# A hybrid decoder layer on one core: late visits of staged pieces in pairs, two more staging buffers, a shorter Newton step, and a residual added by a matrix product

## The chip, the core and the metric

The kernel runs on one core of a Trainium2 chip. A core has TensorE (PE in the profile, with its weight loads as PEld), VectorE (DVE), ScalarE (ACT), GpSimd (POOL) and SyncE (SP); the last three also issue DMAs. The metric is the device time of one execution in microseconds (us); lower is better.

## What is computed

One inference step of a decoder layer, in fp32, for 256 prompt tokens and for 8 sequences with 4 new tokens each (32 decode rows), so 288 tokens in all:

```
h = rms_norm(x, g)                        # 288 x 2048
z = h @ w_in                              # columns of three head groups and their gates
y_conv = silu(c_g) * short_conv(...)      # 512 wide
o_cmp, o_sel, o_win = sparse attention    # 8 heads, 2 kv groups; compressed, selected, window
y_nsa = silu(n_g) * (g0*o_cmp + g1*o_sel + g2*o_win)
y_mem = silu(m_g) * attend(m_q, memory)   # 4 heads, 256 memory tokens
x = x + concat(y_conv, y_nsa, y_mem) @ w_out
y = rms_norm(x, final_g)
```

The 8 decode sequences have 2048 past tokens each in a paged cache, 512 window rows and 256 memory tokens. These are read from HBM once: keys for compression, selected keys and values, window keys and values, memory keys and values. New key and value rows, the updated window and the convolution state are outputs as well.

## The kernel before, in words

**The main stream.** TensorE works through one long list of products of a 1024-column half of a weight tile with the activations (tiles `z`). Each fp32 operand is split into a high part and a rest (`wh` and `wl` for weights), and three of the four partial products are formed, so that one half costs 24 matmuls of 128x128 by 288 columns (`product_half`). A weight half is loaded by GpSimd's DMA queue (`w_load`, L225) into one of five buffers, ScalarE makes `wh` of it and VectorE `wl`. The halves come in the order of `wsrc`: memory projection, input projection, output projection.

**Work between the products.** Every 12 matmuls the program calls `chunk()`, which lets a set of generators each issue a little: softmaxes, transposes, gates, and the visits of staged pieces. The order on every engine is therefore fixed when the program is built. A generator goes on when a small clock `at` says so, which is advanced by estimated costs (`Timed`, `matmul`, `loading`).

**Staged pieces.** The caches of the decode rows come in pieces of 128x1024 (512 KB). `stages` lists them by due time, `load_next` issues a load whenever a buffer is free, and `stage_stream` visits a stage when all four of its pieces are there by the estimate: it runs 16 small matmuls (output 32 rows by 256 columns) and returns the four buffers with `used_up`, which issues the next loads. There are six buffers `st` and, once the prompt's memory attention is over, a seventh in the tile `qk1`. Visits of the second half of the sequences late in the kernel are: selected keys 7 (`selk_use`, tile `sk`), window keys (`wink_use`, `sk` and `sn`), memory values 0 and 1 (`memv_use`, tile `omd`), window values (`winv_use`, tile `od`), selected values 4 to 7 (`selv_use`, `od`). A value visit first transposes the next part of the softmax weights on TensorE (`weights`, tile `pv`) and then multiplies with the part made a visit earlier. The selected values are gathered by GpSimd with an indirect DMA (L584), on the same queue as the weights.

**Order around these visits.** When both halves are through, `dec_out` writes the decode rows of `mixed`, and `split_decode` prepares them. After twelve first passes of the output projection, four weight halves are multiplied the other way round (`first_rows`, tiles `zr`), then the second passes follow.

**The tail.** The last 512 output columns are held by rows: two groups of 128 prompt tokens (`part[0]`, `part[1]`) and the decode rows, folded as 128x128 (`part[2]`, product tile `zd`). For each group the squares are summed, `factors` computes 1/sqrt with ScalarE's Sqrt, VectorE's reciprocal and one Newton step (`rsqrt` with `rest`), ScalarE scales the rows, TensorE spreads the factors over the partitions (`rb`), and VectorE scales the twelve column tiles (`scale_tiles`).

## Time and profile before

| what | value |
|---|---|
| time, median of 3 runs | 613.99 us (611.5 to 619.14) |
| profiled execution, its own time | 616.16 us |
| its span, first to last instruction | 614.4 us |
| granted TensorE clock, mean | 0.996 |
| PE busy | 603.0 us (98%) |
| DVE busy | 461.0 us (75%) |
| ACT busy | 285.3 us (46%) |
| POOL busy | 200.5 us (33%) |
| HBM traffic over the span | 323 GB/s |

Times in the rows are microseconds from the start of the span. A row of the timeline has start, length, engine, line, operation, output<-inputs, shapes, the number of records, and in brackets the engine's idle time ahead of it with what ended it. One fp32 matmul leaves two records, a product matmul of the main stream one. Matmuls are pipelined: the length of a row is longer than its share of the engine, so shares are read from one start to the next. Lines such as L120 or L137 are the helpers that issue a matmul or an operation of VectorE or ScalarE, so that the tile names tell more.

### The profile page before, as it was taken

The page shows a single profiled execution, that of the slowest core. Times are in us where ns is not written, and L with a number is a line of the kernel's source. Part 1 is how long each engine was busy: PE and PEld are TensorE (multiplying, and loading weights), DVE is VectorE, ACT ScalarE, POOL GpSimd, SP SyncE. Part 2 cuts the span into 40 slices and gives each one's busy share as a digit, 9 for nine tenths or more (in the row PEclk, how much of TensorE's full clock was granted, in tenths as well). Part 3 has the DMA queues.
Part 4 walks back from the last instruction along what each step waited for, and adds up shares of the span by engine and source line. Part 5 has one row for each costly group of instructions (what it writes and reads, how often), then busy time and mean ns, then how long its engine had stood idle before and what let it go on. Part 6 is the DMA issues. An engine that isn't in the chain of part 4 may idle for free.

```text
span 614.4 us, 13419 instructions
## 1 busy us (share of the span) xinstructions
PE 603.0 (98%) x4919; PEld 554.0 (90%) x4919; DVE 461.0 (75%) x749; ACT 285.3 (46%) x499; POOL 200.5 (33%) x282
## 2 busy tenths in 40 slices
PE   8999999999999999999999999999999999999997
PEld 5999999989799999989889889899889989889995
DVE  4879899988485779989789888897668733357666
ACT  4755445543355444435334434543543544335552
POOL 2012544533124442433453552323111336222200
PEclk8999999999999999999999999999999999999999
DMA  8999798999968999798878898999899998859834
GB/s 285 394 403 404 258 320 300 345 310 337 365 203 280 370 407 375 250 387 298 310 232 313 284 386 273 309 318 311 289 334 332 336 353 291 288 195 411 281 130 155
DMA packets 76226, 190.85 MB, mean 311 GB/s; under 512 B 8896, under 2 KB 26464, under 8 KB 75904
## 3 DMA queue, kind: packets, MB, share of 16 engines
q0 software_dynamic: 26048, 100.48, 46.0%
q1 hardware_dynamic: 49104, 88.25, 40.4%
q10 hardware_dynamic: 1008, 1.25, 0.6%
q8 instruction: 39, 0.64, 0.4%
q14 instruction: 27, 0.22, 0.1%
HBM read 184.74 MB, written 13.60 MB: 323 GB/s over the span
## 4 chain that ended last, share of the span: by engine, by line
PE 78%; DMA 11%; DVE 8%; issue 2%; SPq 1%; ACT 0%; ACTq 0%; DVEq 0%
PE z L120 56%; DMA st<-ckc 5%; PE zr L120 4%; PE od L120 3%; DMA st<-ckk 3%; PE sk L120 3%; PE zf L120 2%; DVE wl L137 2%; DVE pooled L137 2%; PE acc L120 2%; PE s L120 2%; DMA rx<-xT 1%; DVE st L137 1%; PE pt L125 1%; DMA mraw<-memT 1%
## 5 line engine op out<-in xcount | busy, mean ns | idle before, releaser
L120 PE MATMUL z<-x,wh 128*128 128x288 f32 x1664 | 254.4, 302 | 0.0
L137 DVE TENSOR_TENSOR wl<-w,wh 128x1024 fp32r<-128x1024 f32 x147 | 185.7, 1265 | 84.6 <-PE z L120 34.9
L120 PEld LDWEIGHTS z<-x,wh 128*128 128x128 f32 x1664 | 229.7, 188 | 7.8 <-issue 6.1
L137 ACT ACTIVATE wh<-w 128x1024 fp32r<-128x1024 f32 x148 | 154.3, 1052 | 25.1 <-PE z L120 15.4
L120 PE MATMUL z<-x,wl 128*128 128x288 f32 x832 | 127.2, 295 | 0.3 <-DVE wl L137 0.3
L120 PEld LDWEIGHTS z<-x,wl 128*128 128x128 f32 x832 | 115.7, 188 | 0.8 <-DVE wl L137 0.7
L356 POOL TENSOR_TENSOR st<-st,cst 128x512 f32<-128x512 f32 x63 | 69.3, 1102 | 133.8 <-DVE st L137 49.3
L225 POOL DMA_DIRECT2D w<-w_in x104 | 58.2, 560 | 109.1 <-DVE wl L137 82.4
L137 DVE TENSOR_REDUCE pooled<-st 128x16 f32<-128x1024 f32 x63 | 76.2, 1210 | 5.8 <-POOL st L356 5.8
L137 DVE TENSOR_TENSOR st<-st,cst 128x512 f32<-128x512 f32 x63 | 43.3, 688 | 10.9 <-DMA st<-ckc 10.8
L225 POOL DMA_DIRECT2D w<-w_out x32 | 17.5, 550 | 63.0 <-DVE wl L137 43.1
L584 POOL DMA_INDIRECT st<-ckv,rows_v x26 | 27.1, 1042 | 31.9 <-PE od L120 17.4
L137 ACT ACTIVATE P<-P,nm 128x128 f32<-128x128 f32 (+1 forms) x32 | 14.2, 445 | 29.3 <-DVE nm L137 29.3
L120 PE MATMUL z<-m,wh 128*128 128x256 f32 x192 | 27.3, 287 | 0.5 <-DVE mvt L137 0.5
L120 PE MATMUL z<-y,wh 128*128 128x288 f32 x192 | 27.6, 297 | 0.0
L120 PE MATMUL z<-y1a,wh 128*128 128x288 f32 x168 | 26.7, 299 | 0.0
L120 PEld LDWEIGHTS z<-y,wh 128*128 128x128 f32 x192 | 26.3, 188 | 0.1
L120 PEld LDWEIGHTS z<-y1a,wh 128*128 128x128 f32 x168 | 23.6, 188 | 2.1 <-issue 1.2
L120 PEld LDWEIGHTS z<-m,wh 128*128 128x128 f32 x192 | 24.7, 191 | 0.8 <-issue 0.7
L120 PE MATMUL sk<-st,qz 128*32 128x256 f32 x272 | 20.4, 383 | 1.4 <-DMA st<-ckk 1.2
L120 PE MATMUL od<-st,S 128*32 128x256 f32 x256 | 18.7, 382 | 0.0
L120 PE MATMUL zf<-mixed,w 128*128 128x256 f32 x64 | 16.6, 421 | 1.9 <-DVE mixed L137 1.7
(318 smaller groups left out, 716.2 us busy)
## 6 DMA issues: line engine op xcount, KB each, us to landing
w<-w_in POOLq DMA_DIRECT2D x104, 512.0 KB
st<-ckc SPq DMA_DIRECT2D x126, 256.0 KB, 5.8
w<-w_out POOLq DMA_DIRECT2D x32, 512.0 KB
st<-ckk SPq DMA_DIRECT2D x112, 128.0 KB, 5.1
w<-w_mem SPq DMA_DIRECT2D x12, 512.0 KB, 7.1
o_wk<-wk POOLq DMA_DIRECT2D x8, 512.0 KB
o_wv<-wv POOLq DMA_DIRECT2D x8, 512.0 KB
st<-mv SPq DMA_DIRECT2D x7, 512.0 KB, 7.9
```

The costliest lines, as they stand in the source:

```text
L120: nc.tensor.matmul(out, a, b, **kw)
L125: nc.tensor.transpose(out, a, b)
L137: return getattr(self.engine, name)(*args, **kw)
L225: (nc.gpsimd if s >= ON_SYNC else nc.sync).dma_start(raws[s], wsrc[s])
L356: done.append(eng.tensor_tensor(tm[:, :, kv], tm[:, :, kv], acmp[:, kv].unsqueeze(1).unsqueeze(1).to_broadcast([128, 2, 4, 64]), op=ALU.mu ...
L584: nc.gpsimd.indirect_dma_start(t, None, ckv, bass.IndirectOffsetOnAxis(ap=rows_v[:, j * 4 + b:j * 4 + b + 1], axis=0))
```

## The change

**Pairs.** `HELD` names four stages of the second half. When `stage_stream` reaches one of them it keeps it back and visits it together with the next stage: selected keys 7 with the window keys, memory values 0 with 1, selected values 4 with 5, and 6 with 7. Before a pair of value visits both parts of the softmax weights that it still needs are transposed. The buffers of both stages come free together.

**Two more buffers.** When the prompt's attention is over and the first half of the sequences is decoded, the new keys that are still needed are copied out of `kk` (a VectorE copy of 128x128 into columns 3712 to 3840 of `qk1`), and columns 0 to 1024 and 2176 to 3200 of `qk1` are given to the staging as buffers eight and nine.

**Newton step.** In the tail, the step multiplies r*r by v in one operation of VectorE, where two stood, with the factor -0.5 taken into a second set of constants (`rest` has six columns, written by one more small operation).

**Residual of the decode rows.** The residual `part[2]` is no longer added by VectorE: a matmul with the identity puts it into `zd` ahead of the decode products, and the squares and the gains read `zd` directly.

```diff
--- before.py
+++ after.py
@@ -199,11 +199,15 @@
     def rsqrt(r, ssq, rest=None):
 
         v, t = small(3, "yv", 1)[:, :r.shape[1]], small(3, "yt", 1)[:, :r.shape[1]]
-        act.activation(r, ssq, AF.Sqrt, scale=1.0 / D, bias=C("eps") if rest is None else rest)
-        if rest is None:
-            vec.tensor_scalar(v, ssq, 1.0 / D, EPS, op0=ALU.mult, op1=ALU.add)
-        else:
-            vec.scalar_tensor_tensor(v, ssq, 1.0 / D, rest, op0=ALU.mult, op1=ALU.add)
+        if rest is not None:
+            act.activation(r, ssq, AF.Sqrt, scale=1.0 / D, bias=rest[0])
+            vec.scalar_tensor_tensor(v, ssq, -0.5 / D, rest[1], op0=ALU.mult, op1=ALU.add)
+            vec.reciprocal(r, r)
+            vec.scalar_tensor_tensor(t, r, r, v, op0=ALU.mult, op1=ALU.mult)
+            vec.scalar_tensor_tensor(r, t, 1.5, r, op0=ALU.add, op1=ALU.mult)
+            return
+        act.activation(r, ssq, AF.Sqrt, scale=1.0 / D, bias=C("eps"))
+        vec.tensor_scalar(v, ssq, 1.0 / D, EPS, op0=ALU.mult, op1=ALU.add)
         vec.reciprocal(r, r)
         vec.tensor_tensor(t, r, r, op=ALU.mult)
         vec.scalar_tensor_tensor(t, t, -0.5, v, op0=ALU.mult, op1=ALU.mult)
@@ -481,7 +485,7 @@
             for g in range(2):
                 for b in range(4):
                     matmul(s[32 * b:32 * b + 32, 32 * j:32 + 32 * j], qcols(0, 4 * hf + b, g),
-                                     kk[:, 2 * j + g, 256:288], start=(g == 0), stop=(g == 1), skip_group_check=True)
+                                     kn[hf][:, 2 * j + g], start=(g == 0), stop=(g == 1), skip_group_check=True)
         nmask = C("newmask")[:, hf * 32:(hf + 1) * 32]
         vec.tensor_tensor(S[:, C_NS:C_NS + 32], s[:, 0:32], nmask, op=ALU.add)
         vec.tensor_tensor(S[:, C_NW:C_NW + 32], s[:, 32:64], nmask, op=ALU.add)
@@ -567,7 +571,7 @@
     def values(hf, i, t):
 
         o, PT = env["o"], env["PT", hf, i]
-        if i < 4:
+        if i < 4 and ("PT", hf, i + 1) not in env:
             weights(hf, i + 1)
         t = [x.rearrange("p (n c) -> p n c", n=4) for x in t]
         for n in range(4):
@@ -726,6 +730,7 @@
     tiles_of, ready, place = {}, {}, {}
     buffers = [one.tile([128, 1024], F32, name=f"st{i}") for i in range(NST)]
     free = []
+    HELD = ((selk_use, 7), (memv_use, 0), (selv_use, 4), (selv_use, 6))
     nl = [0]
 
     def load_next():
@@ -747,15 +752,26 @@
 
         last_cmp = 0.0
         needs = {selk_use: "q", memk_use: "mq"}
+        held = []
         for due, f, u, j in stages:
             while (now[0] < due - EARLY or needs.get(u) not in env or len(tiles_of.get((u, j), ())) < pieces(u) or at[0] < ready[u, j]
                    or u is cmp_use and (at[0] < last_cmp + CMP_GAP or at[VEC] > at[0] + BACKLOG)):
                 yield 1
             if u is cmp_use:
                 last_cmp = at[0]
-            yield from u(j, tiles_of.pop((u, j)))
+            if (u, j) in HELD:
+                held.append((u, j))
+                continue
+            if u is selv_use and held:
+                for q in (j % 4 + 1, j % 4 + 2):
+                    if q < 5 and ("PT", j // 4, q) not in env:
+                        weights(j // 4, q)
+            for u, j in (*held, (u, j)) if u is not cmp_use else ((u, j),):
+                yield from u(j, tiles_of.pop((u, j)))
+                if u is not cmp_use:
+                    used_up(u, j)
             if u is not cmp_use:
-                used_up(u, j)
+                held.clear()
 
 
     m_hl = [xhl.tile([128, KT, 256], F32R, name=f"m{n}", tag=f"qk{n}") for n in range(2)]
@@ -1343,6 +1359,12 @@
                 yield from prompt_nsa(g, tt)
                 yield 1
         env["prompt_done"] = True
+        while not env.get(("decoded", 0)):
+            yield 1
+        vec.tensor_copy(kn[1], kk[:, :, 256:NT])
+        for o in (0, 2176):
+            free.append(qk1[:, o:o + 1024])
+            load_next()
 
 
     def then(gen):
@@ -1363,6 +1385,7 @@
     qq = xhl.tile([128, 16, 256], F32, name="qq", tag="qk0")
     qk1 = xhl.tile([128, 4096], F32, name="qk1", tag="qk1")
     kk = qk1[:, 0:4 * NT].rearrange("p (i n) -> p i n", i=4)
+    kn = [kk[:, :, 256:NT], qk1[:, 3712:3840].rearrange("p (i n) -> p i n", i=4)]
     mq = qk1[:, 1152:2176].rearrange("p (h t) -> p h t", h=4)
     vnat = {3: qk1[:, 2176:2688].rearrange("p (s g d) -> p s g d", s=2, g=2),
             5: qk1[:, 2688:3200].rearrange("p (s g d) -> p s g d", s=2, g=2)}
@@ -1528,7 +1551,7 @@
     yo = xhl.tile([128, 4096], F32, name="yo", tag="qk1")
     yod = pbig.tile([128, 1024], F32, name="yod", tag="big")[:, :512]
     out = (yo[:, 0:2048], yo[:, 2048:4096], yod)
-    rest, sums2 = small(3, "yrest", 1), small(3, "ysums", 1)
+    rest, sums2 = small(6, "yrest", 1), small(3, "ysums", 1)
     quarters = small(32, "imp", 1)
     both = zt("A", "both")
     sel, accd = both[:, 0:128], both[:, 128:256]
@@ -1546,18 +1569,21 @@
             for q in range(4):
                 o = (k % 2) * ROWS + 128 * q
                 matmul(zd[32 * q:32 * q + 32, :128], mixed[:, k, 256:NT], wr[k // 2][:, o:o + 128],
-                       start=(k == 0), stop=(k == KT - 1), skip_group_check=True)
-
-    def squares(g, z):
-        vec.tensor_tensor(part[g], z, part[g], op=ALU.add)
-        act.activation(scratch[:, :part[g].shape[1]], part[g], AF.Square, accum_out=sums2[:, g:g + 1])
+                       start=False, stop=(k == KT - 1), skip_group_check=True)
+
+    y_of = [part[0], part[1], zd[:, :128]]
+
+    def squares(g):
+        if g < 2:
+            vec.tensor_tensor(part[g], z[g], part[g], op=ALU.add)
+        act.activation(scratch[:, :part[g].shape[1]], y_of[g], AF.Square, accum_out=sums2[:, g:g + 1])
 
     def gains(g):
-        vec.tensor_tensor(out[g][:, out[g].shape[1] - part[g].shape[1]:], part[g], fgr[g], op=ALU.mult)
+        vec.tensor_tensor(out[g][:, out[g].shape[1] - part[g].shape[1]:], y_of[g], fgr[g], op=ALU.mult)
 
     def factors(g, ssq):
         r = small(1, f"yr{g}", 1)
-        rsqrt(r, ssq, rest[:, g:g + 1])
+        rsqrt(r, ssq, (rest[:, g:g + 1], rest[:, 3 + g:4 + g]))
         return r
 
     def spread_rows(g, r):
@@ -1598,8 +1624,9 @@
     for i, a in enumerate((acc[:, 0:128], acc[:, 128:256], accd)):
         matmul(ssq[:, i:i + 1], a, C("ones"), start=True, stop=True, skip_group_check=True)
     rows(z[0], ws[2], 6, y, 0, False, True)
-    vec.tensor_scalar(rest, ssq[:, 0:3], 1.0 / D, EPS, op0=ALU.mult, op1=ALU.add)
-    squares(0, z[0])
+    vec.tensor_scalar(rest[:, 0:3], ssq[:, 0:3], 1.0 / D, EPS, op0=ALU.mult, op1=ALU.add)
+    vec.tensor_scalar(rest[:, 3:6], ssq[:, 0:3], -0.5 / D, -0.5 * EPS, op0=ALU.mult, op1=ALU.add)
+    squares(0)
     gains(0)
     r0 = factors(0, sums2[:, 0:1])
     scale_rows(0, r0, nc.sync)
@@ -1609,16 +1636,17 @@
     rows(z[1], ws[2], 6, y, 1, False, True)
     scale_tiles(0, 0, 4, nc.sync)
     scale_tiles(0, 4, 8, nc.sync)
-    squares(1, z[1])
+    squares(1)
     scale_tiles(0, 8, 12, nc.sync)
     gains(1)
     r1 = factors(1, sums2[:, 1:2])
     scale_rows(1, r1, nc.scalar)
+    matmul(zd[:, :128], ident, part[2], start=True, stop=False, skip_group_check=True)
     decode_rows(0, SPREAD_AT)
     spread_rows(1, r1)
     decode_rows(SPREAD_AT, KT)
     scale_tiles(1, 0, 4, nc.sync)
-    squares(2, zd[:, :128])
+    squares(2)
     busy(TAIL_BUSY[0])
     matmul(ssq[:, 3:4], sel, sums2[:, 2:3], start=True, stop=True)
     scale_tiles(1, 4, 8, nc.sync)
```

On GpSimd's queue, the weight loads (`w`) and the gathers of selected values (`st` and `qk` from `ckv`) stand as follows before, from the weight loads ahead of the third group of gathers on:

```order
L225 DMA w_6472<-w_out 128x1024
L225 DMA w_6506<-w_out 128x1024
L584 DMA st_105<-ckv,rows_v 128x1024
L584 DMA st_107<-ckv,rows_v 128x1024
L584 DMA st_106<-ckv,rows_v 128x1024
L584 DMA st_109<-ckv,rows_v 128x1024
L225 DMA w_6566<-w_out 128x1024
L225 DMA w_6600<-w_out 128x1024
L584 DMA st_108<-ckv,rows_v 128x1024
L584 DMA st_104<-ckv,rows_v 128x1024
L584 DMA qk_793<-ckv,rows_v 128x1024
L584 DMA st_105<-ckv,rows_v 128x1024
```

With the change, from the fourth weight load after the second group of gathers on:

```order
L229 DMA w_6543<-w_out 128x1024
L229 DMA w_6577<-w_out 128x1024
L588 DMA st_109<-ckv,rows_v 128x1024
L588 DMA st_108<-ckv,rows_v 128x1024
L588 DMA st_104<-ckv,rows_v 128x1024
L588 DMA qk_793<-ckv,rows_v 128x1024
L588 DMA st_105<-ckv,rows_v 128x1024
L588 DMA qk_793<-ckv,rows_v 128x1024 x2
L229 DMA w_6660<-w_out 128x1024
L229 DMA w_6692<-w_out 128x1024
```

Groups of four gathers with two or three weight loads between them have become groups of up to seven, with five weight loads ahead of this one.

On TensorE, the first of the two memory value visits (tile `omd`) stands before between products `z` in this way, and the second follows 60 products later:

```order
L120 MATMUL z_6098<-x_112,wh_6014 128x288
L120 MATMUL z_6098<-x_113,wh_6014 128x288
L120 MATMUL omd<-st_106,qk_793 32x256 x4
L120 MATMUL omd<-st_109,qk_793 32x256 x4
L120 MATMUL omd<-st_108,qk_793 32x256 x4
L120 MATMUL omd<-st_104,qk_793 32x256 x4
L120 MATMUL z_6098<-x_112,wh_6014 128x288
L120 MATMUL z_6098<-x_113,wh_6014 128x288
```

With the change:

```order
L120 MATMUL z_6103<-x_112,wl_6094 128x288 x8
L120 MATMUL omd<-qk_793 32x256 x4
L120 MATMUL omd<-st_107,qk_793 32x256 x4
L120 MATMUL omd<-st_106,qk_793 32x256 x4
L120 MATMUL omd<-st_109,qk_793 32x256 x4
L120 MATMUL omd<-st_108,qk_793 32x256 x4
L120 MATMUL omd<-st_104,qk_793 32x256 x4
L120 MATMUL omd<-qk_793 32x256 x4
L120 MATMUL omd<-st_105,qk_793 32x256 x4
L120 MATMUL z_6219<-x_112,wh_6104 128x288
```

Both visits now stand in one piece, with no product between them, and they come after a full half. The scores against the compressed keys (`sc`, 8 matmuls), which stood right behind the visit of selected keys 7, now stand alone between products, 36 products ahead of the pair of key visits.

At the end of VectorE's list, from the first scaling of the second group's column tiles (`yo` from `ysum` and `rb`) on, there stands before:

```order
L137 TENSOR_TENSOR yo<-ysum,rb 128x512
L137 TENSOR_TENSOR ysum<-zd,ysum 128x128
L137 TENSOR_TENSOR yo<-ysum,rb 128x512
L137 TENSOR_TENSOR yod<-ysum,st_104 128x128
L137 TENSOR_TENSOR yo<-ysum,rb 128x512
L137 SCALAR_TENSOR_TENSOR yv<-ssqy,yrest 128x1
L137 RECIPROCAL yr_7625<-yr_7625 128x1
L137 TENSOR_TENSOR yt<-yr_7625 128x1
L137 SCALAR_TENSOR_TENSOR yt<-yt,yv 128x1
L137 SCALAR_TENSOR_TENSOR yr_7625<-yt,yr_7625 128x1
L137 TENSOR_TENSOR yod<-ysum,rb 128x384
```

With the change:

```order
L137 TENSOR_TENSOR yo<-ysum,rb 128x512 x2
L137 TENSOR_TENSOR yod<-zd,st_104 128x128
L137 TENSOR_TENSOR yo<-ysum,rb 128x512
L137 SCALAR_TENSOR_TENSOR yv<-ssqy,yrest 128x1
L137 RECIPROCAL yr_7625<-yr_7625 128x1
L137 SCALAR_TENSOR_TENSOR yt<-yr_7625,yv 128x1
L137 SCALAR_TENSOR_TENSOR yr_7625<-yt,yr_7625 128x1
L137 TENSOR_TENSOR yod<-ysum,rb 128x384
```

The addition into `ysum` and one operation of the step are gone, and the gain of the decode rows (`yod`) reads `zd`.

## The prediction

> **What bounds the kernel now.** I read the profile's page first, then the busy time by stretches, then the timeline of TensorE where the visits move, then the tail on all engines. The page and the stretches say this:
>
> ```profile
> PE 603.0 (98%) x4919; PEld 554.0 (90%) x4919; DVE 461.0 (75%) x749; ACT 285.3 (46%) x499; POOL 200.5 (33%) x282
> PE z L120 56%; DMA st<-ckc 5%; PE zr L120 4%; PE od L120 3%; DMA st<-ckk 3%; PE sk L120 3%; PE zf L120 2%; DVE wl L137 2%; DVE pooled L137 2%; PE acc L120 2%; PE s L120 2%; DMA rx<-xT 1%; DVE st L137 1%; PE pt L125 1%; DMA mraw<-memT 1%
> 450.00:500.00 50.00, 50.00 (x485) 45.17 (x478) 33.67 (x80) 22.69 (x40) 12.69 (x19) 1.00 0.93 339
> 500.00:550.00 50.00, 50.00 (x419) 44.18 (x418) 20.26 (x21) 21.12 (x33) 18.13 (x25) 1.00 0.75 262
> ```
>
> The reader is to see that TensorE has no idle time from 450 to 550 us (the second and third column: 50.00 of 50.00), where all the moved visits lie, at a granted clock of 1.00, while the DMA engines are busy 93% and 75% of it at 339 and 262 GB/s. There the time is TensorE's list of instructions and what it loses between them. A change of the order can gain only what an entry into a visit and the way back cost; a change of the loads can only lose, by making this list wait. After the last product the chain runs through small operations of VectorE, and these decide the end.
>
> **Pairs of visits.** First the price of a visit, from the starts of rows on TensorE (two records to an fp32 matmul, one to a product):
>
> ```profile
> 523.13 1.22 PE L120 MATMUL z<-y1a,wl 128*128 128x288 f32 x8
> 524.19 0.63 PE L125 MATMUL pv<-cst,S 128*128 128x128 f32 x4
> ...
> 528.86 1.22 PE L120 MATMUL z<-y1a,wl 128*128 128x288 f32 x8
> 529.92 1.90 PE L120 MATMUL z<-y1a,wh 128*128 128x288 f32 x13
> ...
> 533.10 1.90 PE L120 MATMUL z<-y1a,wh 128*128 128x288 f32 x13
> ...
> 535.23 1.22 PE L120 MATMUL z<-y1a,wl 128*128 128x288 f32 x8
> ...
> 536.85 0.58 PE L120 MATMUL od<-st,S 128*32 128x256 f32 x3
> ...
> 537.71 0.58 PE L120 MATMUL od<-st,S 128*32 128x256 f32 x3
> ...
> 540.48 1.22 PE L120 MATMUL z<-y1a,wl 128*128 128x288 f32 x8
> ```
>
> A half of 24 products alone takes 533.10 - 529.92 = 3.18 us. With the visit of selected values 7 in it, which has no transposes, it takes 540.48 - 535.23 = 5.25 us, so that visit costs 2.07 us. In its midst eight matmuls (sixteen records) take 537.71 - 536.85 = 0.86 us, that is 0.1075 each, and sixteen would take 1.72. The rest, 2.07 - 1.72 = 0.35 us, is the price of going in and out once. The visit at 524.19, with four transposes ahead, costs 528.86 - 523.13 - 3.18 = 2.55 us, 0.48 more, for transposes whose row lasts 0.63 in all. So when two visits become one, 0.35 us goes away, and with both sets of transposes put together perhaps 0.05 more.
>
> The Trainium skill gives a reason for such a price: its page "TensorEngine Tiling (Array Packing)", section Key Properties, says "Mode switching requires drain", and a visit's 32-row outputs stand between full 128-row products; the trace agrees in that 0.35 us is lost around a visit, but doesn't show a drain as such.
>
> Three pairs of visits lose one such passage each: memory values 0 and 1, selected values 4 and 5, selected values 6 and 7. That is 3 x 0.35 = 1.05 us. The fourth pair, selected keys 7 with the window keys, loses a passage and gains one, since the compressed scores had none of their own:
>
> ```profile
> 448.24 1.93 PE L120 MATMUL sk<-st,qz 128*32 128x256 f32 x32
> 449.99 0.31 PE L120 MATMUL sc<-kcT,qz 128*32 128x32 f32 x16
> 450.23 2.39 PE L120 MATMUL z<-x,wh 128*128 128x288 f32 x16
> ```
>
> They stand right behind `sk` and take 450.23 - 449.99 = 0.24 us, the way out included. Alone between products they pay for going in and out, at the most the same 0.35 us. I take the pair at nothing; its ends are 0 and -0.35. The last transpose of the decode output (`ot`), which stood between a product and the turned products, comes 24 products earlier and now has products on both sides: I add 0.1 us as an estimate (a third of a passage; ends 0 and 0.35). Products and visits together: -1.05 + 0.1 = -0.95 us, with ends of 0 and -1.6.
>
> **The loads.** The bytes are the same. Nine buffers hold two stages and one piece ahead; eight come free at once, and up to seven gathers stand in GpSimd's list ahead of the next weight load. Their cover is the lead of the weights:
>
> ```profile
> 516.46 0.99 POOL L584 DMA_INDIRECT st<-ckv,rows_v  x1 [4.09 <-PE od L120]
> ...
> 520.43 0.94 POOL L584 DMA_INDIRECT st<-ckv,rows_v  x1 [0.30 <-issue]
> 521.37 1.16 POOL L225 DMA_DIRECT2D w<-w_out  x2
> 530.42 1.05 ACT L137 ACTIVATE wh<-w 128x1024 fp32r<-128x1024 f32 x1
> st<-mv SPq DMA_DIRECT2D x7, 512.0 KB, 7.9
> ```
>
> Three gathers after the first take 520.43 - 516.46 = 3.97 us, 1.32 each. The first weight half issued at 521.37 is the one that ScalarE converts at 530.42 (counted back from the last half on both engines), a lead of 9.05 us and the shortest of the late halves. Three gathers more push such an issue back by up to 4.0 us and leave 5.1. A 512 KB load of SyncE's lands a median of 7.9 us after issue, so the conversion could be 2.8 us late. TensorE wants a converted half two halves (6.4 us) after the conversion's normal start; less 1.05 us for the conversion itself, 5.3 us of cover are left. I therefore cost the loads at nothing on the path; with the cover gone they cost what the rival below works out. Behind a late conversion wait ScalarE's own later work (product evictions, `wh` of the next half) and then VectorE's `wl`.
>
> The Trainium skill's page "DMA: Bandwidth & Descriptors", section SWDGE vs HWDGE vs iDMA, speaks against the change here: for DMAs issued from GpSimd "only 1 is allocated" of queues. By that rule a weight half also stands behind the data of all gathers ahead of it. The row of the weights agrees in the order of issue; no row shows the order of landing.
>
> The copy of the new keys on VectorE (128x128) has the whole stretch up to 455 us as cover, where VectorE is busy 33.67 of 50 us: nothing. If it came late, the window keys' loads would.
>
> **The tail.** These are its rows:
>
> ```profile
> 606.51 0.30 PEld L120 LDWEIGHTS rb<-cst,yr 128*128 128x128 f32 x2 [0.20 <-DVE yr L137]
> ...
> 607.04 0.69 DVE L137 TENSOR_TENSOR yo<-ysum,rb 128x512 f32<-128x512 f32 x1 [0.79 <-PE rb L120]
> ...
> 607.86 0.29 DVE L137 TENSOR_TENSOR ysum<-zd,ysum 128x128 f32<-128x128 f32 x1
> 608.07 0.68 DVE L137 TENSOR_TENSOR yo<-ysum,rb 128x512 f32<-128x512 f32 x1
> 608.19 0.31 ACT L137 ACTIVATE st<-ysum 128x128 f32<-128x128 f32 x1 [1.18 <-DVE ysum L137]
> 608.87 0.68 DVE L137 TENSOR_TENSOR yo<-ysum,rb 128x512 f32<-128x512 f32 x1
> 609.06 0.26 ACT L137 ACTIVATE yr<-ssqy,yrest 128x1 f32<-128x1 f32 x1 [0.47 <-PE ssqy L120]
> 609.47 0.15 DVE L137 SCALAR_TENSOR_TENSOR yv<-ssqy,yrest 128x1 f32<-128x1 f32 x1
> 609.53 0.15 DVE L137 RECIPROCAL yr<-yr 128x1 f32<-128x1 f32 x1
> 609.72 0.16 DVE L137 TENSOR_TENSOR yt<-yr 128x1 f32<-128x1 f32 x1
> 609.91 0.16 DVE L137 SCALAR_TENSOR_TENSOR yt<-yt,yv 128x1 f32<-128x1 f32 x1
> ```
>
> From 607.04 VectorE has no gap worth naming until the step for the decode rows. Without the addition into `ysum` the next `yo` starts behind the first, at 607.04 + 0.61 (the spacing of neighbours, 609.47 - 608.87 = 0.60) = 607.65 instead of 608.07: -0.42 us. The step has one operation less: 609.91 - 609.72 = -0.19. What is late next is ScalarE's path: its square starts where VectorE's addition did (607.86 instead of 608.19), so the Sqrt moves from 609.06 to 608.73 and ends at 608.99, when the reciprocal would want it at 609.53 - 0.42 = 609.11. So the gain is just kept whole. The shorter step for the second group is worth up to 0.19 at 606.51, where TensorE's weight load waits 0.20 us for it, but the identity matmul stands ahead of the decode products on TensorE: a transpose of the same size takes 0.63 / 4 = 0.16. I take these two together at -0.1, with ends of +0.2 (0.3 for the matmul, as an estimate of twice its row) and -0.2. For the first group TensorE has the second group's products right behind, and I count nothing. The second set of constants is one operation of 0.15 us ahead of a wait of VectorE for the products: nothing. Tail: -0.42 - 0.19 - 0.1 = -0.7 us, ends -0.3 and -0.9.
>
> **Sum.** -0.95 - 0.7 = -1.65 us. Against the profiled execution's own 616.16 us (span 614.4 and 1.8 around it) this is 614.5; that execution lies 2.2 us above the median of the runs shown, 613.99, and the same step from the median gives 612.3 us. That is my forecast.
>
> **Rivals.** *The passages cost nothing that can be saved:* the 0.35 us could belong to each visit's own first and last matmuls, which a pair still has per accumulation. Then only the tail is left: 613.3 us. For it speaks that the price was never seen without a visit; against it that inside a visit the matmuls run at an even 0.1075 us. The Trainium skill would back this rival: "TensorE: Matmul & The Clock Gate", section Step-by-step: what each phase is for, says that the drain of one matmul overlaps the fill of the next; by that rule a passage is nearly free, and the trace's 0.35 us speaks against it. Chance 0.15.
>
> *The weights come late behind a burst of gathers:* seven gathers and two weight halves, nine pieces of 0.52 MB, share the DMA engines at the 262 GB/s of that stretch, 2.0 us each, so that the weight lands up to 18 us after the burst begins. It was due with 5.1 us of lead behind 9 us of issuing, about 14 us after the begin; 18 less 14 and less the 5.3 us of cover is no stall, but a window copy of another two pieces in the same place makes it 22 us, 2.7 us late; the same at the memory pair, where seven loads must land within 108 products (14.3 us), makes another 1 to 2 us. Then 612.3 + 4 = 616.3 us, slower than before. It decides from the point at which a weight takes over about 10.4 us (5.1 + 5.3) from issue to landing. Against it speaks that TensorE shows no wait with groups of four. Chance 0.13.
>
> *The tail doesn't show at the end,* since the last output DMA, not VectorE, closes the span: 613.0 us. Against it: the last column tiles are issued behind VectorE's last operation. Chance 0.1. *My forecast* has 0.62.
>
> **Range and chances.** The forecast's own ends are 614.0 - 2.5 and 614.0 - 0.3; three executions shown spread from 2.5 below to 5.1 above their median, so I allow another 2.3 on either side: 609.2 to 616.3, which also holds the rivals' times. A measurement of this kernel tells about 2% (12 us) from no change. No case reaches 12 us faster, and only the weights' rival, several times over, 12 us slower: faster 0.01, same 0.97, slower 0.02.
>
> **What would show it.** Right: in the timeline one piece of 64 records of `omd`, and pairs of `od`, each 0.35 us cheaper than two visits; the last product half of the turned products starting about 1 us earlier; TensorE still busy 50.00 of 50.00; the last `yod` 1.65 us earlier. Wrong: waits of `z` for `wl` or `wh`, or of `omd`, `od` or `sk` for a DMA, or ScalarE's `wh` waiting for a weight's DMA between 450 and 545 us; or a Sqrt that ends after `yv`.

## The result and the profile after

The changed kernel took 619.94 us (median of 22 runs, 616.76 to 624.37) against 614.21 us for the kernel before beside it: a ratio of 1.0098, 95% interval 1.0077 to 1.0118. It was 5.7 us slower where 1.65 us less was forecast, and outside the forecast's range of 609.2 to 616.3. By the bound of 2% that is "same". On two chips, numbers 3 and 13, the same kernel was later 0.3% to 0.5% *faster* than before; which chip the first measurement ran on is not recorded. The experiments below come to that.

The profiled execution of the changed kernel took 618.97 us (span 617.1). First the page's line of busy times and the busy time by stretches, to set beside those of before. A stretch's columns are its length, then busy time and instructions of TensorE, its weight loads, VectorE, ScalarE and GpSimd, then the granted clock, the DMA engines' busy share and GB/s.

```profile
PE 605.1 (98%) x4921; PEld 557.3 (90%) x4921; DVE 459.7 (74%) x747; ACT 285.5 (46%) x499; POOL 200.9 (33%) x282
470.00:485.00 15.00, 15.00 (x150) 13.22 (x149) 9.26 (x25) 6.10 (x12) 7.08 (x9) 1.00 0.90 333
485.00:490.00 5.00, 2.95 (x18) 2.67 (x17) 4.56 (x10) 2.44 (x5) 0.71 (x2) 0.84 0.97 386
490.00:495.00 5.00, 5.00 (x29) 4.40 (x27) 2.11 (x4) 1.96 (x3) 0.39 (x1) 0.82 0.84 266
515.00:520.00 5.00, 5.00 (x61) 4.10 (x50) 0.00 (x0) 0.00 (x0) 3.80 (x4) 1.00 0.53 156
520.00:525.00 5.00, 3.90 (x30) 3.67 (x29) 0.98 (x1) 1.03 (x2) 3.46 (x5) 1.00 0.85 302
```

TensorE now stands idle twice between 450 and 550 us, where it had been busy without a gap: 2.05 us behind 485 us, with a granted clock of 0.84 and 0.82 in the stretches around and after it (cut finer, 0.50 from 488.5 to 491.8 us and 1.00 again after that), and 1.1 us before 525. From 515 to 520 us VectorE and ScalarE are busy 0.00 us: nobody evicts a product.

The timelines of the engines in the first of these places (start, duration, engine, line, operation; in brackets the idle time ahead and what ended it):

```profile
478.14 0.27 PE L125 MATMUL otm<-cst,odr 128*128 128x128 f32 x1
...
488.48 0.48 PE L125 MATMUL pe<-cst,odr 128*128 128x128 f32 x1 [2.05 <-DVE odr L137]
...
475.55 1.12 DVE L137 SCALAR_TENSOR_TENSOR odr<-omd,cst,odr 128x128 f32<-128x128 f32 x3
481.70 1.23 DVE L137 TENSOR_TENSOR wl<-w,wh 128x1024 fp32r<-128x1024 f32 x1 [5.02 <-PE z L120]
...
488.13 0.29 DVE L137 TENSOR_TENSOR odr<-S,cst 128x128 f32<-128x128 f32 x1
...
481.67 0.28 ACT L137 ACTIVATE mixed<-otm 128x128 f32<-128x128 f32 x1 [5.22 <-PE z L120]
...
474.43 1.00 POOL L588 DMA_INDIRECT st<-ckv,rows_v  x1 [0.39 <-PE omd L120]
...
479.51 0.94 POOL L588 DMA_INDIRECT st<-ckv,rows_v  x1 [0.30 <-issue]
480.45 0.58 POOL L229 DMA_DIRECT2D w<-w_out  x1
```

VectorE's `wl` waits for the half product that gives way to `otm` at 478.14 us, and ScalarE's copy (`mixed`) waits for `otm` itself, 0.1 us later. Both go on only at 481.7, over 3 us late and 0.03 us apart, though TensorE has long been on its next half. Behind this `wl` stand VectorE's softmax steps, and the last of them, `odr` at 488.13, is what TensorE waits 2.05 us for. From 474.43 to 480.45 us GpSimd issues the five gathers that the pair of memory values set free, and then a weight load until 481.03.

The second place, the same views:

```profile
519.98 1.90 PE L120 MATMUL z<-y1a,wh 128*128 128x288 f32 x13
...
524.43 1.74 PE L120 MATMUL z<-y1a,wh 128*128 128x288 f32 x11 [1.10 <-issue]
...
523.97 0.41 ACT L137 ACTIVATE ysum<-z 128x288 f32<-128x288 f32 x1 [9.22 <-PE z L120]
...
524.02 1.22 DVE L137 TENSOR_TENSOR wl<-w,wh 128x1024 fp32r<-128x1024 f32 x1 [10.50 <-PE z L120]
...
515.28 0.99 POOL L588 DMA_INDIRECT st<-ckv,rows_v  x1 [4.13 <-PE od L120]
...
522.85 0.94 POOL L588 DMA_INDIRECT qk<-ckv,rows_v  x1 [0.30 <-issue]
```

A half gives way to the next at 519.98 us; its eviction (`ysum`) starts at 523.97, 4.0 us later, just behind the last of seven gathers. The other `z` buffer is full by then, and TensorE stops for 1.10 us. The kernel before had a like lateness once, in a row of four gathers, without a wait of TensorE:

```profile
500.00 1.22 PE L120 MATMUL z<-y1a,wh 128*128 128x288 f32 x8
...
501.65 0.41 ACT L137 ACTIVATE ysum<-z 128x288 f32<-128x288 f32 x1 [4.64 <-PE z L120]
```

There the eviction came 1.65 us after the next half had started.

So the question is what makes VectorE and ScalarE learn so late that TensorE is done. An engine tells the others of finished work by raising a counter, its semaphore, for which they wait. The trace also notes when each of TensorE's counts arrives. Set beside the recorded end of the matmul that sends it (for a half some 0.16 us after the next one starts), this gives, for the changed kernel:

```
matmul that signals   its end (us)   count noted (us)   late (us)   gathers issued meanwhile
last of omd                474.88          475.02          0.14     first of five
half before otm            478.30          481.62          3.31     fourth, fifth, and a weight load
otm                        478.42          481.65          3.23     the same
od, last of the pair       516.75          518.10          1.35     second, third of seven
half                       520.14          523.94          3.80     fifth to seventh
half                       523.33          525.56          2.23     seventh, and two weight loads
```

Outside GpSimd's rows of gathers the counts come 0.01 to 0.12 us after the end. ScalarE's and VectorE's own counts, where the trace notes them, come at most 0.03 us after their operation.

But the trace doesn't note all of them. Between 200 and 600 us this profile lacks 26 counts of the three engines, all in GpSimd's rows of gathers or within 1.5 us behind one. The nine other profiles in which counts of TensorE come late lack 20 to 32, and those of chips 3 and 13 further below lack none. A missing count need not be a late one: that of the eviction which ends at 523.97 + 0.41 = 524.38 us is missing, and TensorE goes on at 524.43, which may be why the profile names no engine for its wait of 1.10 us. So in these rows two things go together: late counts of TensorE, and counts that are missing from the trace.

For comparing kernels I use two lengths, which leave out what comes before them: the *late stretch*, from the first product behind the last `acc` to the first `ssqy`, and the *end*, from there to VectorE's last `yod`. Both have the same work in all kernels here, except for the steps changed. Before: 156.25 and 14.51 us. Changed kernel, this profile: 160.38 and 14.07 us.

### The profile page after: what moved, and what is told of

It is laid out like the page before. It is cut to its first block, busy times and chain, and to the rows that moved or that the text cites. A ratio compares the mean times of both kernels' runs of the same rounds, so it can differ in the third digit from the quotient of the medians.

```text
span 617.1 us, 13424 instructions
## 1 busy us (share of the span) xinstructions
PE 605.1 (98%) x4921; PEld 557.3 (90%) x4921; DVE 459.7 (74%) x747; ACT 285.5 (46%) x499; POOL 200.9 (33%) x282
## 5 line engine op out<-in xcount | busy, mean ns | idle before, releaser
L588 POOL DMA_INDIRECT st<-ckv,rows_v x22 | 23.4, 1065 | 19.1 <-PE od L120 7.4
L120 PE MATMUL zf<-mixed,w 128*128 128x256 f32 x64 | 18.6, 456 | 1.2 <-DVE mixed L137 1.1
L120 PEld LDWEIGHTS zf<-mixed,w 128*128 128x128 f32 x64 | 14.4, 231 | 5.8 <-DVE mixed L137 3.5
```

The source lines that it names most:

```text
L120: nc.tensor.matmul(out, a, b, **kw)
L588: nc.gpsimd.indirect_dma_start(t, None, ckv, bass.IndirectOffsetOnAxis(ap=rows_v[:, j * 4 + b:j * 4 + b + 1], axis=0))
```

## Experiments

Theory A: signals of TensorE are late while GpSimd issues rows of gathers, and the pairs make the rows longer. Rival B: weights or pieces land late behind the gathers. Rival C: the new order itself holds up VectorE and ScalarE. Rival D: the end has become slower. The changed kernel was not run beside the first eight kernels, all on chip 12, so that their ratios to the kernel before, and their late stretches, have to be compared with its first measurement.

**The end alone.** Only the edits of the end, in the kernel before:

```diff
+            vec.scalar_tensor_tensor(t, r, r, v, op0=ALU.mult, op1=ALU.mult)
+            vec.scalar_tensor_tensor(r, t, 1.5, r, op0=ALU.add, op1=ALU.mult)
...
+    matmul(zd[:, :128], ident, part[2], start=True, stop=False, skip_group_check=True)
```

> The kernel before with only the end of the change: Newton step in two operations, decode residual by a product with the identity; loads and visits as before. Theory A (signals of TensorE come late while GpSimd issues a long row of gathers; the end is as forecast) expects 0.5 to 0.7 us less than before, ratio 0.999. Rival B (weights or pieces land late behind the gathers) and rival C (the pairs' order itself holds up VectorE and ScalarE) expect the same. Rival D (the lost time is at the end) expects 3 to 6 us more than before, ratio 1.005 to 1.010.

Ratio 0.9986 (0.995 to 1.0021). The interval alone would not exclude a small loss, but the profile does: a late stretch of 156.25 us as before and an end of 14.06 us, 0.45 less. D falls.

**No pairs.**

```diff
-    HELD = ((selk_use, 7), (memv_use, 0), (selv_use, 4), (selv_use, 6))
+    HELD = ()
```

> The changed kernel with an empty list of held visits: both new buffers and the new end stay, each visit stands alone again. GpSimd's list then has gathers of four, eight and three in a row, eight where two visits follow each other. Theory A expects a late signal behind the row of eight and some 2 to 4 us more than before, ratio 1.003 to 1.007. Rival C expects the time of the end alone, 0.5 us less than before, ratio 0.999. Rival B (two more buffers pull loads ahead of weights) expects 2 to 6 us more too.

Ratio 0.9981 (0.9953 to 1.0009), late stretch 156.97 us. The ratio is near that of rival C, which the next run refutes, and below what theory A and rival B expected. There are late signals, up to 2.47 us, but only one wait of TensorE, of 0.57 us: how late a signal is doesn't tell what it costs. Buffers and end without pairs don't make the kernel slower.

**Plain loads for the late gathers.** Here the selected values of the second half are fixed rows, not the selected ones.

```diff
+        if j > 3:
+            nc.gpsimd.dma_start(t, ckv[128 * (4 * j + b):128 * (4 * j + b) + 128])
+            return
```

> The changed kernel where the late gathers (second half of the selected values) are plain loads of the same bytes on the same queue of GpSimd, of fixed rows and not of the selected ones; the selected values of these sequences are therefore wrong ones. The order of TensorE is that of the changed kernel, and so is GpSimd's list. Theory A expects the waits of 0.5 and 1.1 us on TensorE and the clock dip gone: 1.5 us less than before, ratio 0.997 to 0.998. Rival B (order and bytes of the loads) and rival C (order of VectorE and ScalarE) expect the time of the changed kernel, ratio 1.008 to 1.010.

Ratio 0.9975 (0.9942 to 1.0009); late stretch 155.33 us, no late signal in it. The timelines of GpSimd, VectorE and ScalarE at the first place:

```profile
472.39 1.66 POOL L589 DMA_DIRECT2D st<-ckv  x3 [0.15 <-PE omd L120]
474.05 0.53 POOL L589 DMA_DIRECT2D qk<-ckv  x1
474.64 0.53 POOL L589 DMA_DIRECT2D st<-ckv  x1
475.16 0.53 POOL L229 DMA_DIRECT2D w<-w_out  x1
...
476.58 1.23 DVE L137 TENSOR_TENSOR wl<-w,wh 128x1024 fp32r<-128x1024 f32 x1 [1.70 <-PE z L120]
...
476.63 0.28 ACT L137 ACTIVATE mixed<-otm 128x128 f32<-128x128 f32 x1 [1.98 <-PE otm L125]
```

The same `wl` now waits 1.70 us and not 5.02. TensorE's order is that of the changed kernel, and so are the bytes, the queue and the lists of all engines: C falls, and of B what comes from bytes and order. But a plain load takes 0.53 us to issue, so the row is over before the half ends; the run doesn't tell whether a plain row of the same length would hold signals too.

**Gathers two at a time.**

```diff
+PACE = 2
...
+            if f is selv_load and j > 3:
+                if now[0] < pace[0]:
+                    return
+                pace[1] += 1
+                if pace[1] % PACE == 0:
+                    pace[0] = now[0] + 2
```

> The changed kernel where late gathers are issued two at a time, the next two at the earliest 24 products later, so that weight loads stand between them; the pairs of visits stay, the last of them six products later. Theory A expects most of the lost time back: between 1.5 us less and 1 us more than before, ratio 0.997 to 1.002. Rival B expects the same, since weights are no longer behind long rows. Rival C expects the time of the changed kernel, ratio 1.008 to 1.010.

Ratio 0.998 (0.9945 to 1.0014), late stretch 155.25 us, the latest signal in it 0.34 us. GpSimd and VectorE at the first place:

```profile
474.49 0.97 POOL L589 DMA_INDIRECT st<-ckv,rows_v  x1 [0.30 <-issue]
475.46 0.59 POOL L230 DMA_DIRECT2D w<-w_out  x1
476.36 0.97 POOL L589 DMA_INDIRECT st<-ckv,rows_v  x1 [0.30 <-issue]
...
477.15 1.22 DVE L138 TENSOR_TENSOR wl<-w,wh 128x1024 fp32r<-128x1024 f32 x1 [1.73 <-PE z L121]
```

The pairs, and the gathers as gathers, are kept, with weight loads between them; the rows are cut, and `wl` waits 1.73 us, as with plain loads.

**One kind of pair at a time.**

```diff
-    HELD = ((selk_use, 7), (memv_use, 0), (selv_use, 4), (selv_use, 6))
+    HELD = ((selv_use, 4), (selv_use, 6))     # selv_pairs
+    HELD = ((memv_use, 0),)                   # memv_pair
```

> The changed kernel with the two pairs of selected values alone; memory values and the last selected keys stand by themselves. GpSimd's rows of gathers are then of four, four and seven. Theory A (TensorE's signals come late in long rows of gathers; the row of five behind the memory pair costs the 2.05 us wait and the clock dip, some 3.5 us, the row of seven 1.1 us) expects between 1 us less and 1 us more than before, ratio 0.998 to 1.002, with a late signal left in the row of seven. If it is the selected pairs themselves that cost, 1.005 to 1.010.

> The changed kernel with the pair of memory values alone. GpSimd's list has gathers of five, eight (two visits that follow each other closely) and three. Theory A expects the wait behind the row of five again: 2 to 4 us more than before, ratio 1.003 to 1.007. If the memory pair is harmless, the time of the kernel without pairs, ratio 0.998.

Selected pairs alone: ratio 0.9992 (0.9956 to 1.0028), late stretch 156.94 us. Around its row of seven signals are still up to 3.76 us late, at a price of one wait of TensorE of 0.63 us. Memory pair alone: 1.003 (1.000 to 1.006), late stretch 160.18 us, with the wait of the first place again:

```profile
491.35 0.47 PE L125 MATMUL pe<-cst,odr 128*128 128x128 f32 x1 [2.12 <-DVE odr L137]
...
484.58 1.23 DVE L137 TENSOR_TENSOR wl<-w,wh 128x1024 fp32r<-128x1024 f32 x1 [5.03 <-PE z L120]
...
477.30 1.00 POOL L588 DMA_INDIRECT st<-ckv,rows_v  x1 [0.39 <-PE omd L120]
```

Most of what the late stretch gained in length is therefore behind the memory pair: its row of five gathers ahead of a `wl` that stands before the softmax steps. The two ratios alone would not tell, since their intervals overlap.

**Weights from SyncE's queue.**

```diff
+LATE_SYNC = 120
...
-                (nc.gpsimd if s >= ON_SYNC else nc.sync).dma_start(raws[s], wsrc[s])
+                (nc.gpsimd if ON_SYNC <= s < LATE_SYNC else nc.sync).dma_start(raws[s], wsrc[s])
```

> The changed kernel where the weight halves of the output projection are loaded from SyncE's queue and no longer from GpSimd's behind the gathers. All gathers and visits as in the changed kernel. Rival B (weights late behind the gathers) expects the lost time back, ratio 0.997 to 1.000. Theory A expects the waits on TensorE to stay and the time of the changed kernel, ratio 1.007 to 1.010.

Ratio 1.0015 (0.9984 to 1.0046), late stretch 158.17 us: between what rival B and theory A expected. The first place has no late signal here; the second is worse than in the changed kernel (TensorE, ScalarE, GpSimd):

```profile
518.28 1.90 PE L121 MATMUL z<-y1a,wh 128*128 128x288 f32 x13
...
524.17 2.04 PE L121 MATMUL z<-y1a,wh 128*128 128x288 f32 x13 [1.28 <-ACT ysum L138]
...
523.71 0.41 ACT L138 ACTIVATE ysum<-z 128x288 f32<-128x288 f32 x1 [10.66 <-PE z L121]
...
513.58 0.94 POOL L589 DMA_INDIRECT st<-ckv,rows_v  x1 [13.86 <-PE od L121]
...
521.05 0.94 POOL L589 DMA_INDIRECT qk<-ckv,rows_v  x1 [0.31 <-issue]
```

A product that was done at 518.28 is evicted at 523.71, 5.4 us late, and no weight stands in GpSimd's list; behind the gathers it issues copies of the window. An eviction reads no weight at all. B falls for the second place. That the first went quiet was not foreseen, and for that place B is refuted only by the plain loads, which left the weights in GpSimd's queue.

**No gather waits for TensorE.**

```diff
+        n = min(len(free), len(loads) - nl[0])
+        if n and loads[nl[0]][0] is selv_load and loads[nl[0]][2] > 3:
+            for t in free[:n]:
+                nc.gpsimd.memset(t[:, 0:1], 0.0)
```

> The changed kernel where, ahead of each row of late gathers, GpSimd clears one column of each of their buffers: the clearing takes the wait for TensorE, and no gather itself waits for TensorE any more. Same gathers, rows and bytes. Theory A1 (TensorE's signal is held while a gather that waits on that very signal is handled) expects the late signals gone and 1 to 1.5 us less than before, ratio 0.997 to 0.999. Theory A2 (the signals are late whatever the gathers wait for) expects the time of the changed kernel, ratio 1.007 to 1.010.

The trace is on the side of A2: signals are late by 3.36 us in the row of five and 2.85 in the row of seven, the wait for `odr` is 2.09 us, the late stretch 160.23 us. The time is on neither side: 1.0000 (0.9966 to 1.0033), though the late stretch is that of the changed kernel. So it isn't the gather's own wait on TensorE's semaphore, and one profiled execution does not give the size of the loss in the timed ones.

**Which buffer is filled first.** In the two late places a release that one of the row's instructions waits for comes after the row's first gather has begun: `omd` ends at 474.88 us and the first of five gathers starts at 474.43. Theory A3 makes that the cause. The buffer that a visit frees last is filled first; `FIX` names the rows, all three in `last_first`, that of five in `lf_row1`, that of seven in `lf_row3`. The fourth run is the changed kernel itself.

```diff
+            if f is selv_load and first:
+                first = False
+                if j in FIX:
+                    free.insert(0, free.pop())
...
         free.extend(place.pop((u, j)))
-        load_next()
+        if not more:
+            load_next()
```

`more` is set for the first visit of a pair.

> The changed kernel where in each late row of gathers the buffer that a visit frees last is filled first, and a pair's eight buffers are given out together; so only a row's first gather waits for TensorE, and by then every buffer of the row is free. Rows of five, four and seven gathers and the pairs stay; the last pair comes twelve products later. Theory A3 (TensorE's signals are held back when the release that a queued gather waits for arrives while another gather is being issued, and then until about the end of the row) expects no late signal, no wait of TensorE, and 1 to 1.6 us less than before, ratio 0.997 to 0.999. Theory A2 (long rows hold signals whatever they wait for) expects the time of the changed kernel, 1.007 to 1.010.

> The same, for the row of five behind the memory pair alone. Theory A3 expects the wait of 2.05 us for the window weights and the clock dip behind it gone, those behind the row of seven left: 1 to 3 us more than before, ratio 1.002 to 1.005, and 3.5 us less than the changed kernel.

> The same, for the row of seven behind the pair of selected values 4 and 5 alone. Theory A3 expects the wait of 1.1 us gone and that of 2.05 us left: 2 to 4 us more than before, ratio 1.003 to 1.007.

> The changed kernel itself, beside these three on the same chip: 1.008 to 1.010 by all theories.

Ratios 1.0003 (0.9983 to 1.0022), 0.9973 (0.9951 to 0.9995), 0.9982 (0.9948 to 1.0015), and for the changed kernel itself **0.9962 (0.9943 to 0.998)**: 0.4% faster than before, "same" by the bound of 2%. The eight kernels above had run on one chip, number 12; these four ran on another, number 3, and none of their traces has a signal that is over 0.12 us late, in no row of gathers, not even in the early ones near 290 us, where traces of chip 12 have 0.4 to 2.7 us. So three of these runs tested nothing of what they were made for, and the fourth overturned what all theories had foreseen. At the second place in the changed kernel on chip 3 (from a later run, `after_fifth`):

```profile
518.66 1.90 PE L120 MATMUL z<-y1a,wh 128*128 128x288 f32 x13
...
518.86 0.41 ACT L137 ACTIVATE ysum<-z 128x288 f32<-128x288 f32 x1 [5.43 <-PE z L120]
...
513.97 0.99 POOL L588 DMA_INDIRECT st<-ckv,rows_v  x1 [4.13 <-PE od L120]
...
519.04 1.92 POOL L588 DMA_INDIRECT st<-ckv,rows_v  x1 [0.31 <-PE z L120]
```

The same row of seven gathers is under way, and the eviction follows the end of its half by 0.20 us.

**The changed kernel again, for the tie between late signals and time.**

> The changed kernel itself once more. Theory A: where the trace shows signals of TensorE that come over 2 us late within rows of gathers, TensorE waits as in the first measurement and the ratio is 1.007 to 1.010; where it shows none, 0.995 to 0.998 as in the run before. A rival, that chips differ in something else and the late signals don't matter, expects no such tie.

> The kernel that fills the last-freed buffer first, beside the changed kernel on the same chip. Theory A3 (a signal is held when the release that a queued gather waits for comes while another gather is issued) expects 0.997 to 1.000 and no late signal, on either kind of chip. Theory A2 (long rows hold signals whatever they wait for) expects the ratio of the changed kernel where signals are late.

> The changed kernel itself once more. Theory A: where the trace shows signals of TensorE that come over 2 us late within rows of gathers, ratio 1.007 to 1.010; where it shows none, 0.993 to 0.998 as in the two runs before.

> The kernel that fills the last-freed buffer first, beside the changed kernel on the same chip. On a chip with late signals theory A3 expects none in this kernel and 0.997 to 1.000, theory A2 the late signals and the ratio of the changed kernel; on a chip without, both expect 0.997 to 1.001.

> The kernel before itself, for its profile beside that of the changed kernel: ratio 1.000. All theories expect that TensorE does not wait between 450 and 550 us; on a chip without late signals ScalarE's and VectorE's start at 501.65 and 501.71 us, 1.65 us behind the half product they wait for, comes at 0.2 us behind it.

> The changed kernel beside it. Theory A: 0.993 to 0.998 where the trace shows no late signal, and of the gain some 1 us between the last compressed scores and the turned products and some 0.7 us at the end; 1.007 to 1.010 where signals come over 2 us late.

The changed kernel: 0.9949 (0.992 to 0.9977) on chip 3, 0.9964 (0.9935 to 0.9993) on chip 13, 0.9969 (0.9946 to 0.9992) on chip 3. The kernel with the last-freed buffer first: 0.999 (0.9967 to 1.0013) and 0.9978 (0.9947 to 1.0009). The kernel before against itself: 1.0024 (0.9992 to 1.0056), which shows what a ratio here is worth: 0.2% either way means little. None of these traces has a late signal.

All in one table (times in us; late: by how much the latest signal of TensorE between 455 and 530 us came after its matmul; the rows up to `no_pe_wait` are from chip 12, or, in the first two, from traces with late signals whose chip is not recorded):

```
kernel           ratio (95%)               late stretch   end     late
before           1                         156.25         14.51   1.46
changed          1.0098 (1.0077, 1.0118)   160.38         14.07   3.80
tail_only        0.9986 (0.9950, 1.0021)   156.25         14.06   1.44
no_pairs         0.9981 (0.9953, 1.0009)   156.97         14.06   2.47
plain_loads      0.9975 (0.9942, 1.0009)   155.33         14.07   0.12
paced            0.9980 (0.9945, 1.0014)   155.25         14.06   0.34
selv_pairs       0.9992 (0.9956, 1.0028)   156.94         14.06   3.76
memv_pair        1.0030 (1.0000, 1.0060)   160.18         14.06   3.39
weights_sync     1.0015 (0.9984, 1.0046)   158.17         14.05   5.24
no_pe_wait       1.0000 (0.9966, 1.0033)   160.23         14.06   3.36
                 chips 3 and 13
before_again     1.0024 (0.9992, 1.0056)   156.19         14.52   0.12
after_again      0.9962 (0.9943, 0.9980)   155.33         14.05   0.12
after_third      0.9949 (0.9920, 0.9977)   155.32         14.06   0.12
after_fourth     0.9964 (0.9935, 0.9993)   155.33         14.06   0.12
after_fifth      0.9969 (0.9946, 0.9992)   155.32         14.07   0.12
last_first       1.0003 (0.9983, 1.0022)   155.51         14.08   0.05
last_first_2     0.9990 (0.9967, 1.0013)   156.04         14.07   0.05
last_first_3     0.9978 (0.9947, 1.0009)   155.87         14.07   0.05
lf_row1          0.9973 (0.9951, 0.9995)   155.53         14.06   0.12
lf_row3          0.9982 (0.9948, 1.0015)   155.82         14.07   0.07
```

The late stretch of the changed kernel is 155.32 or 155.33 us in four executions on two chips without late signals, and 160.38 in the one with them.

What stays open: the changed kernel was not met again on a chip with late signals, so that its first result, 1.0098, stands alone; its own profile explains 160.38 - 156.25 - 0.44 = 3.7 us of the 5.7. On chip 12 the traces say more than the times: the slowest kernel with late signals, `memv_pair` at 1.0030 (1.0000 to 1.0060), overlaps `paced` at 0.9980 (0.9945 to 1.0014), and `no_pe_wait` is at 1.0000. That late signals stop TensorE is shown in the profiled executions; that they make up the 1% of the first measurement is argued. And since the same traces lack counts, the recording itself may have a part in the lateness, which no run tests. Nor was filling the last-freed buffer first tried on such a chip. A3 has a row against it, too: in the kernel with the end alone, the row of four gathers from 314.5 us begins after the visit that frees its buffers, and signals are up to 1.48 us late in it. What makes TensorE's signals late on one chip and not on another, no run shows.

## Why the prediction was right or wrong

**The step that failed** is the one under "The loads": that they cost nothing on the path. It weighed only whether a weight would land late, and gave the row of up to seven gathers a cover of 5.3 us against that. In the profile of the first measurement the late stretch is 160.38 - 155.33 = 5.05 us longer than the 155.33 us without late signals on chips 3 and 13, by another way: while GpSimd issued the rows of five and seven, ScalarE and VectorE learned 2 to 4 us late that TensorE was done. TensorE's two waits are 2.05 and 1.10 us of this, and the lower clock behind the first about 1.5. The rival that stood for a loss was right about the place, the bursts of gathers at the memory pair and the selected pairs, and its 616.3 us was nearer than the forecast. That is luck, because its mechanism isn't what the trace shows: no `wh` waits for a weight's DMA there, and with no weight behind the gathers the second place got worse. The sign was in the trace of before: the eviction at 501.65 behind a half that was over at 500.00, in a row of four gathers. I had looked only at whether TensorE waited there.

**Where no signal is late the forecast's steps hold in the main.** Summed, the profiles of chip 3 give 155.32 - 156.19 = -0.87 us for products and visits (forecast -0.95) and 14.07 - 14.52 = -0.45 us for the end (forecast -0.7): -1.3 us in place of -1.65. The four ratios on chips 3 and 13, 0.995 to 0.997, are 2 to 3 us; what they have beyond 1.3 us isn't placed, and the part ahead of the late stretch, where this profile of before ends at 445.57 and those of the changed kernel at 434.92 to 442.02, varies by more than that from one execution to the next.

*Pairs.* Forecast 0.35 us for each passage saved. TensorE's rows around the memory values, `before_again` and then `after_fifth`:

```profile
464.23 2.35 PE L120 MATMUL z<-x,wh 128*128 128x288 f32 x16
...
489.20 0.27 PE L125 MATMUL otm<-cst,odr 128*128 128x128 f32 x1
```

```profile
459.08 0.78 PE L120 MATMUL z<-x,wh 128*128 128x288 f32 x4
...
480.57 0.27 PE L125 MATMUL otm<-cst,odr 128*128 128x128 f32 x1
```

Before, 489.20 - 464.23 = 24.97 us hold both visits and 156 products; after, 480.57 - 459.08 = 21.49 us hold the pair and 132. The 24 products that are missing take 3.18: 24.97 - 21.49 - 3.18 = 0.30 us saved. The same reckoning gives 0.30 and 0.34 for the two pairs of selected values, and nothing for the selected keys with the window keys, whose passage the compressed scores take over, as foreseen. So the rival by which a passage costs nothing falls. The page "TensorEngine Tiling (Array Packing)" of the Trainium skill, section Key Properties, says that a change of tiling mode drains TensorE; the trace agrees in that a third of a microsecond goes with each passage, but shows no drain as such.

*The end.* VectorE's and TensorE's rows, `before_again` and then `after_fifth`:

```profile
611.99 0.69 DVE L137 TENSOR_TENSOR yo<-ysum,rb 128x512 f32<-128x512 f32 x1 [0.78 <-PE rb L120]
...
615.07 0.16 DVE L137 SCALAR_TENSOR_TENSOR yr<-yt,yr 128x1 f32<-128x1 f32 x1
...
607.93 0.63 PE L120 MATMUL zr<-wl_last,y 128*128 128x512 f32 x2
...
611.47 0.49 PE L120 MATMUL rb<-cst,yr 128*128 128x128 f32 x2
```

```profile
607.67 1.28 DVE L137 TENSOR_TENSOR yo<-ysum,rb 128x512 f32<-128x512 f32 x2 [1.14 <-PE rb L120]
...
609.95 0.22 DVE L137 SCALAR_TENSOR_TENSOR yt<-yr,yv 128x1 f32<-128x1 f32 x1
610.20 0.16 DVE L137 SCALAR_TENSOR_TENSOR yr<-yt,yr 128x1 f32<-128x1 f32 x1
...
603.39 0.63 PE L120 MATMUL zr<-wl_last,y 128*128 128x512 f32 x2
...
607.14 0.49 PE L120 MATMUL rb<-cst,yr 128*128 128x128 f32 x2
```

From the first `yo` behind `rb` to the last step of the factor it was 615.07 - 611.99 = 3.08 us and is 610.20 - 607.67 = 2.53: 0.55 gained of the 0.42 + 0.19 forecast, since the fused operation lasts 0.22 us and not 0.16. The term that was mis-sized is the one of the identity matmul, taken at -0.1 with the shorter step: from the last product to the second `rb` it was 611.47 - 607.93 = 3.54 us and is 607.14 - 603.39 = 3.75, 0.21 *more*, the upper end that I had given it (+0.2). The remaining 0.1 us of the gain lies ahead of these rows, around the first group's step, where I had counted nothing. The Sqrt keeps up, as foreseen. The end does show at the end, since the span closes 3.1 us behind the last `yod` in both profiles (619.4 - 616.27 and 614.5 - 611.41): that rival falls too.

*The copy of the new keys* shows in no wait.

**The range** was built from the forecast's own terms, and the one rival for a loss got 0.13. With rows of gathers made up to seven long in a kernel where a row of four already delayed an eviction, it should have had more. Two ends are also added up wrongly: 614.0 - 0.3 + 2.3 is 616.0, while 616.3 is the rival's time, and the tail's own terms, -0.61 with +0.2 and -0.2, end at -0.4 and -0.8. Neither would have reached 619.94.

## What to carry to other kernels

Before lengthening a row of gathers on GpSimd, look in the trace for evictions that start long after the end of the product they wait for: here such a delay cost nothing at 1.65 us, while TensorE still had the other `z` buffer, and stopped TensorE at 4.0 us. Cut such rows (two gathers, then other work) rather than let a joined visit free eight buffers at once: the paced kernel kept the pairs and had no such wait on a chip that showed late signals. And a loss of 1% in one measurement was a gain of 0.3% to 0.5% in four others: before explaining it, measure again, note the chip, and look whether one trace shows something that others don't, missing records among it.

## What was not expected of the hardware

On chip 12, and in the first measurement, counts of TensorE's semaphore reached the trace up to 5.24 us after the matmul that sent them, always in or just behind rows of gathers issued by GpSimd; on chips 3 and 13, with the same program and the same rows, 0.12 us at most. The traces with late counts also lack 20 to 32 counts of the three engines in these rows, the others none. Where counts were late, ScalarE and VectorE started 0.02 to 0.1 us behind the noted count. The Trainium skill's page "Perfetto Trace Analysis", section Tensor Engine Instruction (MATMUL, LD_WEIGHTS), says that a matmul's end in a profile is an estimate and that the update is pushed once PSUM, where products are written, has acknowledged all bytes and then has to propagate; the traces agree in that the end alone doesn't tell when others learn of it, but whether the acknowledgement or the propagation was late they do not show.

A wait of TensorE of 2.05 us was followed by a granted clock of 0.50 over the next 3.4 us (488.5 to 491.8), in which products, `pe` and `pv` took 1.5 us more than in an undisturbed execution (5.43 us from `pe` to the next `od`, against 3.90 in `after_fifth`). The memory pair alone and `no_pe_wait` show the same 0.50 behind waits of 2.12 and 2.09 us. The length of a wait alone doesn't decide: behind the waits of 1.10 us in the changed kernel and 1.28 us in `weights_sync` the clock stayed at 1.00, but so it did in `weights_sync` behind one of 2.47 us that ended at 161.61, while in `after_fifth` it was 0.50 from 160.0 to 163.2, behind one of 1.48 us.
